# Sixteen of 31 convolution taps moved from VectorE to TensorE in a two-block fp32 model

## The chip, the cores and the metric

The kernel runs on one core of a Trainium2 chip. The metric is the device time of one launch in microseconds (us). Five engines run beside each other, each working through its own list of instructions in order: TensorE (PE; its weight loads are PEld), VectorE (DVE), ScalarE (ACT), GpSimd (POOL) and SyncE (SP), which only issues DMAs. An instruction that waits holds up all that stand behind it on its engine.

## The reference

Batch 1, 512 tokens (T), 1024 features, fp32. Two layers of a first block (each a mixer and a feed-forward part) are followed by one layer of a second block (two attention branches and a feed-forward part). The change touches the mixer's convolution branch alone:

```python
u = h @ w_in                                   # 1024 -> 4096
x_m, z, glu_a, glu_b = split(u, 4)             # 1024 channels each
...                                            # x_m, z: an mLSTM with 4 heads
a = glu_a * sigmoid(glu_b)
a = causal_depthwise_conv(a, w_dw, b_dw)       # 31 taps, each channel by itself
a = silu(group_layer_norm(a, 8, g_cn, b_cn))   # 8 groups of 128 channels
y = concat([h_m, a]) @ w_out
```

The convolution gives y[t] = b + sum over d = 0 to 30 of w[30 - d] * a[t - d], for each of 1024 channels.

## The kernel before

Products keep fp32 accuracy by splitting each operand into a rounded part and a remainder. `mm3` (L197 to L199) issues three matmuls for one product; a 128x512 result needs 24 of them. A weight unit is fetched by SP into one of two raw buffers `wr` (`fetch`, L170), rounded on ACT (L177) and its remainder taken on POOL (L179) or DVE (L68, through a helper that records all its instructions there), into one of four buffers `w`.

The order of the work is made in two steps. The code issues TensorE's products one after another and keeps a rough clock for TensorE (`pt`) and for VectorE (`dt`). After each product `pump` issues work in the background (generators that yield a cost on VectorE, an earliest time and a condition) while VectorE would not fall more than `slack` us behind TensorE. A list scheduler then fixes each engine's order by priorities; `later("tap")` puts the taps behind other work of VectorE.

In the mixer, feature tile c of the convolution (128 channels by 512 tokens, 8 tiles a layer) goes this way. Two products give glu_a and glu_b. ACT takes the tanh (L906), DVE writes the gated input `ga` (tile of three buffers). `conv_gen` (L819 to L832) has ACT write tap 0 with the bias into a bank of PSUM (L825; tag `py`, two banks), and DVE adds taps 1 to 30 there, one instruction each (L830). `conv_out` (L834 to L869) then copies the bank to SBUF (ACT, L839), turns it on TensorE (L846), takes the statistics and an inverse root on DVE (tile `cc`), norms on ACT (L858), turns it back on TensorE (L862) and applies the silu. The mLSTM's gates use fp32 matmuls without the split (`gates_mm`, L633): 128x32 weights by 512 columns into one of four groups of 32 PSUM partitions. Each such fp32 matmul shows as two rows in the trace. The 96 sums for the modulation (`ada_sum`, L287; 1024 columns each on VectorE, their tiles fetched by SP in the first mixer, by POOL after it) are background work of the first mixer and the first feed-forward part.

Of the kernel before, what the change touches and what calls it, by code (L numbers as in the profile page):

```python
# [7 lines left out]
F32 = mybir.dt.float32  # L8
# [9 lines left out]
KC, KM = 31, 4  # L18
EPS = 1e-6
# [11 lines left out]
COLS = {}  # L31
_o = 0
for _n, _w in (("g_pre_mix", 8), ("g_post_mix", 8), ("g_pre_mlp", 8), ("g_post_mlp", 8),
               ("b_ada", 48), ("w_conv_m", 8 * KM), ("b_conv_m", 8), ("g_mh", 8),
               ("w_dw", 8 * KC), ("b_dw", 8), ("g_cn", 8), ("b_cn", 8)):
    COLS[_n] = (_o, _w)
    _o += _w
NCOLS = _o
CONSTS = {"ident": (0, 128), "tri": (128, 128), "fold": (256, 8)}
NCONST = 264  # L40
# [4 lines left out]
# the guess is 1.5 ** 0.2 / sqrt, for the cubic step to have a leading coefficient of 1  # L45
# [8 lines left out]
class Paced:  # L54
    """an engine whose instructions are counted, by their rough time"""
# [16 lines left out]
class Kern:  # L72
    def __init__(self, ctx, tc, A, out, dump=None, stop=None):
# [13 lines left out]
        self.bufs = dict(E=8, s=12, e=1, t=5, tc=3, w=4, wr=2, hT=2, ga=3, z=2, c=26, cc=20, d=10, ad=4, j=2, gw=1, ga16=1)  # L87
# [44 lines left out]
    def pump(self):  # L132
        """issue what fits in before VectorE would be later than TensorE"""
# [12 lines left out]
    def drain(self, done):  # L146
        """issue background work until done()"""
# [11 lines left out]
    def add_chunk(self, src, widths, pool=""):  # L159
        """pool: which of the remainders GpSimd computes"""  # L160
        o = 0
        for i, w in enumerate(widths):
            self.plan.append((src[:, o:o + w], w, str(i) in pool))
            o += w
# [50 lines left out]
    def rsqrt(self, src, w, mul, add, tag=None):  # L215
        """1 / sqrt(src * mul + add), src [128, w]: a guess from the bits, a cubic and a quadratic step"""
# [30 lines left out]
    def setup(self):  # L247
# [8 lines left out]
        self.ones = self.K("tri")[:, 127:128].to_broadcast([128, 128])  # L256

    def load_cols(self, l):
# [10 lines left out]
        for n in ("w_conv_m", "b_conv_m", "w_dw", "g_cn", "b_cn", "g_mh"):  # L269
# [14 lines left out]
    def ada_sum(self, w, l, i):  # L284
        """mod[:, i] = w . silu(c), w the i-th 128 rows of w_ada^T"""
# [32 lines left out]
    def scale_cols(self, l, which):  # L318
        """g_pre * (1 + sc), and sh"""
# [7 lines left out]
    def gate_row(self, l, which):  # L327
        """gt * g_post, as a row on every partition"""
# [17 lines left out]
    def start(self, evacs):  # L346
        """the first normed operand by feature tile, as its scale and shift arrive, and the first products with it"""
# [91 lines left out]
    def norm_T(self, ii, xs, ss, G, sh, to):  # L439
        """rows of the token tiles from ii on, normed; transposed, scaled and split into hT two by two, as pend is worked off"""  # L440
# [48 lines left out]
    def feat(self, evacs, halves=False, hook=None, tag="p"):  # L489
        """128 outputs each: [128, T] = w^T h^T, handed to its evac"""  # L490
# [58 lines left out]
    def post_norm(self, l, which, nxt):  # L549
        """x += gt * rms_norm(y) * g_post; then the next normed operand"""  # L550
# [40 lines left out]
    def gate_weights(self, l):  # L591
        """Wq Wgq + Wk Wgk and Wv Wgv by head, as [feature, 8 gates]; in 4 steps"""
# [46 lines left out]
    def gates(self, l):  # L639
        """gate pre-activations by token -> log forget sums, and what the weights need; in 4 steps"""  # L640
# [89 lines left out]
    def weights_exp(self, h):  # L730
        """exp(a_s - M_t) for s <= t, by key tile"""
# [41 lines left out]
    def values(self, S, vt, h):  # L773
        """weighted sums of values, normed by head: [128 tokens, 4 tiles, 256]"""
# [41 lines left out]

    def conv_gen(self, l, inp, out):
        """the taps of the depthwise convolution, by channel tile"""
        nc, V = self.nc, self.nc.vector  # L819
        for c in range(8):  # L820
            yield 0, 0, lambda: c in inp and self.conv_out_at >= c - 1
            a, w = inp[c], self.cols[l]
            o = COLS["w_dw"][0] + c * KC + KC - 1
            y = self.bank(tag="py")
            nc.scalar.activation(y, a, AF.Identity, scale=w[:, o:o + 1], bias=self.col(l, "b_dw", c))  # L825
            yield 0, self.pt + 1, None
            for d in range(1, KC):
# [6 lines left out]
    def conv_out(self, l, c, yp, outs):  # L834
        """silu(norm over the 128 channels of the group)"""
# [3 lines left out]
        nc.scalar.activation(y, yp, AF.Copy)  # L839
# [220 lines left out]
    def tok_proj(self, n, kks, evac):  # L1060
        """[128 tokens, n] = h w for each token tile"""
# [27 lines left out]
    def rotate(self, src, i, n, pool=False):  # L1089
        """rotary embedding of n heads of token tile i; src and result [128, n, 64]"""  # L1090
# [14 lines left out]
    def q_hold(self, i, p, hold, tag):  # L1105
        """query heads of a token tile, rotated: [tokens, head, rounded part and remainder]"""
# [6 lines left out]
    def q_turn(self, i, hold, qt, hps):  # L1113
        """token tiles i and i + 1 of two pairs of heads into qt"""
# [18 lines left out]
    def q_proj(self, tag):  # L1133
        """8 query heads: 4 tiles [rounded part; remainder of a head, 2 heads, T], once the turns are worked off"""
# [5 lines left out]
    def k_proj(self):  # L1140
        """index key, 2 + 2 key heads: [part twice; T] for the rounded part and the remainder"""
# [61 lines left out]
    def qk_mm(self, out, q, h, tk, k, keys):  # L1203
        """q . k from [q_h; q_l] and [k_h; k_h], [k_l; k_l]"""
# [24 lines left out]
    def select(self):  # L1229
        """in place of the scores: 0 for each query's 128 largest (the earliest among equals), NEG elsewhere"""  # L1230
# [423 lines left out]
```

## Time and profile before

| | |
|---|---|
| time, median of 3 runs (lowest, highest) | 2427.93 us (2426.18, 2431.47) |
| profiled execution, first to last instruction | 2424.3 us |
| PE busy | 2252.7 us, 93% |
| DVE busy | 1610.0 us, 66% |
| ACT, POOL busy | 976.7 us, 625.4 us |
| matmul records | 10552 |

The page gives the profiled execution by its span, 2424.3 us; 3.6 us less than the median of the runs, which take in what lies around the span. In time the stages are: the start (0 to about 60 us), the first mixer (to about 464), its norm and feed-forward part (to 845), a norm (to about 890), the second mixer (to 1277), its norm and feed-forward part (to 1658), the second block's attention (to 2060) and feed-forward part. Busy shares over the whole span mix these stages; the rows below are by stage.

### The profile page before, as it was taken

The numbers are of one execution on the slowest core, as the hardware profiler recorded it, in microseconds if no ns is written. First come the engines' busy times: TensorE is split into PE (matmuls) and PEld (weight loads), VectorE is DVE, ScalarE is ACT, GpSimd is POOL, SyncE is SP. The second block draws the span as 40 slices with busy tenths as digits, with TensorE's granted clock in tenths as the row PEclk, the third lists the DMA queues.
The fourth block names the chain that finished last, engine by engine and source line by source line (L and its number), as shares of the span: only waits on it lengthen the run. The fifth ranks groups of instructions, "written<-read, shape, count | busy, mean of one in ns | idle before, by whom it ended". The sixth has DMA issues, their size and how long they took to land.

```text
span 2424.3 us, 28416 instructions
## 1 busy us (share of the span) xinstructions
PE 2252.7 (93%) x10552; PEld 1828.9 (75%) x10552; DVE 1610.0 (66%) x2971; ACT 976.7 (40%) x1705; POOL 625.4 (26%) x408
## 2 busy tenths in 40 slices
PE   5988998899999998898897999999989999999998
PEld 4667776688888776776676888887877888888886
DVE  6899999755777669999956233347887435443444
ACT  3434554443232343455445333234436543422332
POOL 2733452313234243444322011012031231000000
PEclk9999999999999999999998999999999999999999
DMA  7523223526666422222133332223111223322222
GB/s 271 174 75 106 71 81 118 181 97 214 214 206 205 144 97 81 66 66 66 63 108 104 122 104 96 96 87 109 62 70 44 63 103 138 110 95 94 95 96 87
DMA packets 77754, 271.34 MB, mean 112 GB/s; under 512 B 9008, under 2 KB 9776, under 8 KB 77616
## 3 DMA queue, kind: packets, MB, share of 16 engines
q1 hardware_dynamic: 69840, 241.21, 29.9%
q0 software_dynamic: 7776, 28.32, 3.6%
q8 instruction: 83, 1.36, 0.2%
q14 instruction: 55, 0.45, 0.1%
HBM read 256.91 MB, written 12.58 MB: 111 GB/s over the span
## 4 chain that ended last, share of the span: by engine, by line
PE 62%; DVE 24%; ACT 4%; issue 2%; POOL 1%; DMA 1%; ACTq 0%; DVEq 0%; SPq 0%; POOLq 0%
PE p L197 19%; PE p L199 19%; PE p L198 19%; DVE p L830 7%; DVE c L68 5%; DVE cc L68 2%; DVE t L68 2%; DVE s L68 1%; DVE E L68 1%; PE p L466 1%; DVE w L68 1%; DVE e L68 1%; DVE ad L287 1%; DVE d L68 1%; DVE hT L68 0%
## 5 line engine op out<-in xcount | busy, mean ns | idle before, releaser
L179 POOL TENSOR_TENSOR w<-wr,w 128x1024 fp32r<-128x1024 f32 (+1 forms) x166 | 399.7, 2411 | 842.8 <-ACT w L177 739.3
L177 ACT ACTIVATE w<-wr 128x1024 fp32r<-128x1024 f32 (+1 forms) x353 | 368.9, 1047 | 572.1 <-PE p L199 517.2
L197 PE MATMUL p<-hT,w 128*128 128x512 f32 (+1 forms) x1504 | 582.7, 389 | 14.0 <-ACT hT L209 7.6
L198 PE MATMUL p<-hT,w 128*128 128x512 f32 (+1 forms) x1504 | 576.0, 383 | 8.0 <-DVE hT L68 5.6
L199 PE MATMUL p<-hT,w 128*128 128x512 f32 (+1 forms) x1504 | 578.1, 385 | 1.3 <-POOL w L179 1.3
L197 PE MATMUL p<-w,s 128*128 128x512 f32 (+1 forms) x1152 | 450.9, 392 | 2.4 <-ACT s L209 2.2
L198 PE MATMUL p<-w,s 128*128 128x512 f32 (+1 forms) x1152 | 449.4, 390 | 2.0 <-DVE w L68 2.0
L199 PE MATMUL p<-w,s 128*128 128x512 f32 (+1 forms) x1152 | 447.3, 390 | 1.1 <-DVE s L68 0.8
L68 DVE TENSOR_TENSOR w<-wr,w 128x1024 fp32r<-128x1024 f32 (+1 forms) x187 | 232.9, 1245 | 288.2 <-ACT w L177 288.1
L197 PEld LDWEIGHTS p<-hT,w 128*128 128x128 f32 x1504 | 289.5, 193 | 74.5 <-ACT hT L209 9.6
L830 DVE SCALAR_TENSOR_TENSOR p<-ga,ad,p 128x495 f32<-128x495 f32 (+25 forms) x480 | 339.2, 728 | 3.3 <-ACT p L825 2.3
L198 PEld LDWEIGHTS p<-hT,w 128*128 128x128 f32 x1504 | 289.3, 192 | 64.9 <-DVE hT L68 7.5
L199 PEld LDWEIGHTS p<-hT,w 128*128 128x128 f32 x1504 | 289.3, 192 | 59.4 <-POOL w L179 3.3
L197 PEld LDWEIGHTS p<-w,s 128*128 128x128 f32 x1152 | 217.6, 189 | 52.3 <-ACT s L209 2.9
L199 PEld LDWEIGHTS p<-w,s 128*128 128x128 f32 x1152 | 217.4, 189 | 51.0 <-DVE s L68 1.2
L198 PEld LDWEIGHTS p<-w,s 128*128 128x128 f32 x1152 | 217.4, 189 | 49.6 <-DVE w L68 2.5
L68 DVE TENSOR_TENSOR E<-p,E 128x512 f32<-128x512 f32 (+4 forms) x152 | 95.3, 639 | 138.2 <-PE p L199 111.8
L68 DVE SCALAR_TENSOR_TENSOR t<-p,t 128x512 f32<-128x512 f32 x96 | 66.0, 687 | 129.6 <-ACT t L1028 129.6
L287 DVE SCALAR_TENSOR_TENSOR ad<-ad,ad 128x1024 f32<-128x1024 f32 x80 | 115.5, 1450 | 39.2 <-DMA ad<-in_ada_dram 39.1
L1028 ACT ACTIVATE t<-p 128x512 f32<-128x512 f32 x96 | 56.7, 591 | 179.7 <-PE p L199 179.7
L68 DVE TENSOR_TENSOR s<-t,s 128x512 fp32r<-128x512 f32 (+1 forms) x100 | 110.9, 1109 | 9.5 <-ACT s L1030 4.7
L573 POOL TENSOR_TENSOR E<-E,s 128x512 f32<-128x512 f32 x32 | 46.0, 1445 | 175.2 <-ACT j L571 175.2
(273 smaller groups left out, 2805.2 us busy)
## 6 DMA issues: line engine op xcount, KB each, us to landing
wr<-in_ff_dram SPq DMA_DIRECT2D x128, 512.0 KB, 3.7
wr<-in_win_dram SPq DMA_DIRECT2D x64, 512.0 KB, 3.6
ad<-in_ada_dram POOLq DMA_DIRECT2D x54, 512.0 KB, 4.8
wr<-in_wout_dram SPq DMA_DIRECT2D x40, 512.0 KB, 3.6
wr<-in_up_dram SPq DMA_DIRECT2D x32, 512.0 KB, 3.6
wr<-in_down_dram SPq DMA_DIRECT2D x32, 512.0 KB, 3.7
ad<-in_ada_dram SPq DMA_DIRECT2D x26, 512.0 KB, 4.2
xd<-E SPq DMA_DIRECT2D x20, 512.0 KB, 2.7
```

Of the source, the lines that this page charges most:

```text
L68: return f(out, *a, **kw)
L177: self.nc.scalar.activation(u[:, 0, :w], raw[:, :w], AF.Copy)
L179: eng.tensor_tensor(u[:, 1, :w], raw[:, :w], f32(u[:, 0, :w]), op=OP.subtract)
L197: mm(out, lh, rh, start=first, stop=False)
L198: mm(out, lh, rl, start=False, stop=False)
L199: self.mm = mm(out, ll, rh, start=False, stop=last)
L287: return self.nc.vector.scalar_tensor_tensor(w, w, 1.0, self.cact, op0=OP.mult, op1=OP.mult, accum_out=m)
L466: nc.tensor.transpose(p[:, k, 128 * t:128 * t + 128], x[t][:, j * 128:(j + 1) * 128], self.ident)
L573: nc.gpsimd.tensor_tensor(y[:, h], y[:, h], row[:, h], op=OP.mult)
L830: V.scalar_tensor_tensor(y[:, d:], a[:, :T - d], w[:, o - d:o - d + 1], y[:, d:], op0=OP.mult, op1=OP.add)
L1028: nc.scalar.activation(r, p, AF.Relu)
```

## The change

For each tile, SP copies `ga` 16 times from SBUF to SBUF into a new tile `shifts` [128, 4, 512]: for each of 4 shifts d and each of 4 groups g of 32 channels, partitions 32d to 32d + 31 of column block g get the group's 32 channels, d tokens late. `shifts` is one buffer for all tiles. POOL builds `cw` (two buffers), 16 blocks of 128x32: a stack of four 32x32 identities times the tap weights. Then 16 fp32 matmuls follow (4 sets m of 4 groups g; 128x32 weights by 512 - 4m columns), each for four taps of 32 channels, into the group's 32 partitions of the `py` bank. VectorE adds taps 16 to 30 behind them. ACT no longer writes tap 0; the bias moves into the copy of `conv_out`. The buffer from which POOL's DMAs take their descriptors shrinks to 2048 bytes a partition, which makes room for `shifts`. The rest of the diff takes out comments and docstrings, so line numbers shift by a few.

```diff
+CSETS = 4
+KV = KC - 4 * CSETS
...
-               ("w_dw", 8 * KC), ("b_dw", 8), ("g_cn", 8), ("b_cn", 8)):
+               ("w_dw", 8 * KV), ("w_pe", 32 * CSETS), ("b_dw", 8), ("g_cn", 8), ("b_cn", 8)):
...
+        self.shifts = self.const.tile([128, 4, T], F32, name="shifts")
+        nc.gpsimd.memset(self.shifts[:, :, 0:4], 0.0)
...
+    def conv_pe(self, l, inp, ys):
+        nc = self.nc
+        for c in range(8):
+            yield 0, 0, lambda: c in inp
+            for d in range(4):
+                for g in range(4):
+                    nc.sync.dma_start(self.shifts[32 * d:32 * d + 32, g, d:], inp[c][32 * g:32 * g + 32, :T - d])
+            w = self.tile("cw", (128, 4 * CSETS, 32))
+            nc.gpsimd.tensor_tensor(w, self.K("eye")[:, None, :].to_broadcast([128, 4 * CSETS, 32]),
+                                    self.col(l, "w_pe", c * 4 * CSETS, 4 * CSETS)[:, :, None].to_broadcast([128, 4 * CSETS, 32]),
+                                    op=OP.mult)
+            yield 0, self.pt + 6, lambda: self.conv_out_at >= c - 1
+            y = self.bank(tag="py")
+            for m in range(CSETS):
+                for g in range(4):
+                    nc.tensor.matmul(y[32 * g:32 * g + 32, 4 * m:], w[:, 4 * m + g, :], self.shifts[:, g, :T - 4 * m],
+                                     start=m == 0, stop=m == CSETS - 1)
+            self.pt += 0.853 * CSETS
+            ys[c] = y
+
     def conv_gen(self, l, inp, out):
-        nc, V = self.nc, self.nc.vector
+        V = self.nc.vector
+        ys = {}
+        self.spawn(self.conv_pe(l, inp, ys), front=True)
         for c in range(8):
-            yield 0, 0, lambda: c in inp and self.conv_out_at >= c - 1
-            a, w = inp[c], self.cols[l]
-            o = COLS["w_dw"][0] + c * KC + KC - 1
-            y = self.bank(tag="py")
-            nc.scalar.activation(y, a, AF.Identity, scale=w[:, o:o + 1], bias=self.col(l, "b_dw", c))
+            yield 0, 0, lambda: c in ys
             yield 0, self.pt + 1, None
-            for d in range(1, KC):
+            a, w, y = inp[c], self.cols[l], ys[c]
+            o = COLS["w_dw"][0] + c * KV + KC - 1
+            for d in range(4 * CSETS, KC):
                 yield 0.06 + (T - d) / 860, 0, None
                 with self.later("tap"):
                     V.scalar_tensor_tensor(y[:, d:], a[:, :T - d], w[:, o - d:o - d + 1], y[:, d:], op0=OP.mult, op1=OP.add)
...
-        nc.scalar.activation(y, yp, AF.Copy)
+        nc.scalar.activation(y, yp, AF.Identity, bias=self.col(l, "b_dw", c))
...
-    nc = bacc.Bacc("TRN2", target_bir_lowering=False, num_devices=1)
+    nc = bacc.Bacc("TRN2", target_bir_lowering=False, num_devices=1, dynamic_dma_scratch_size=2048)
```

The scheduler decides where the new instructions land. TensorE, first mixer, the product of glu_a for the third tile, before (`p_925`; `hT` and `w` are its split operands):

```order
L197 MATMUL p_925<-hT_66,w_749 128x512
L198 MATMUL p_925<-hT_67,w_749 128x512
L199 MATMUL p_925<-hT_66,w_749 128x512
L197 MATMUL p_925<-hT_66,w_749 128x512
L198 MATMUL p_925<-hT_67,w_749 128x512
```

The same product now (`p_985`; L199 to L201 are the three matmuls), with the second tile's convolution (`p_889`, L838) in it:

```order
L838 MATMUL p_889<-shifts,cw_836 32x512 x2
L200 MATMUL p_985<-hT_67,w_774 128x512
L201 MATMUL p_985<-hT_66,w_774 128x512
L199 MATMUL p_985<-hT_66,w_774 128x512
L838 MATMUL p_889<-shifts,cw_836 32x512
L200 MATMUL p_985<-hT_67,w_774 128x512
L201 MATMUL p_985<-hT_66,w_774 128x512
L199 MATMUL p_985<-hT_66,w_774 128x512
L838 MATMUL p_889<-shifts,cw_836 32x512
L838 MATMUL p_889<-shifts,cw_836 32x508 x4
L838 MATMUL p_889<-shifts,cw_836 32x504 x4
L838 MATMUL p_889<-shifts,cw_836 32x500 x4
```

The first set of four stands in three pieces (2, 1 and 1 matmuls), three matmuls of the product between them; only the other three sets follow in one piece.

SP's list about there, before (`wr` are weight units, `ad` tiles of the modulation):

```order
L170 DMA wr_786<-in_qkv_dram 128x512
L298 DMA ad_3568<-in_ada_dram 128x1024
L170 DMA wr_847<-in_win_dram 128x1024
L170 DMA wr_923<-in_win_dram 128x1024
L170 DMA wr_1005<-in_win_dram 128x1024
```

And now, with the copies of the second tile (`ga_809`):

```order
L829 DMA shifts<-ga_809 32x512
L172 DMA wr_814<-in_qkv_dram 128x512
L829 DMA shifts<-ga_809 32x512 x3
L829 DMA shifts<-ga_809 32x511 x4
L829 DMA shifts<-ga_809 32x510
L172 DMA wr_877<-in_win_dram 128x1024
L829 DMA shifts<-ga_809 32x510 x3
L829 DMA shifts<-ga_809 32x509 x4
```

Sixteen copies stand between or ahead of the weight fetches of the same time.

VectorE in the first mixer, before, where the taps of two tiles (`p_792`, `p_461`) alternate:

```order
L830 SCALAR_TENSOR_TENSOR p_792<-ga_781,ad_91,p_792 128x511
L830 SCALAR_TENSOR_TENSOR p_461<-ga_421,ad_91,p_461 128x488
L830 SCALAR_TENSOR_TENSOR p_792<-ga_781,ad_91,p_792 128x510
L830 SCALAR_TENSOR_TENSOR p_461<-ga_421,ad_91,p_461 128x487
L68 SCALAR_TENSOR_TENSOR t_835<-E_832,ad_91,t_835 128x511
```

And the second tile's taps now (`p_889`), beginning with tap 16, between sums of the modulation (L291):

```order
L856 SCALAR_TENSOR_TENSOR p_889<-ga_809,ad_93,p_889 128x496
L291 SCALAR_TENSOR_TENSOR ad_784,mod_104<-ad_784,ad_90 128x1024
L856 SCALAR_TENSOR_TENSOR p_889<-ga_809,ad_93,p_889 128x495
L291 SCALAR_TENSOR_TENSOR ad_845,mod_104<-ad_845,ad_90 128x1024
L856 SCALAR_TENSOR_TENSOR p_889<-ga_809,ad_93,p_889 128x494
```

Of the modulation's tiles SP now fetches 43 in the first mixer instead of 26, POOL 37 instead of 54: as many sums move from the feed-forward part into the mixer.

## Rows read from the trace of the kernel before

**Rows 1.** Busy time by stretch; columns in the first row, (x) counts instructions.
```profile
core 0: us, PE busy (x) PEld busy (x) DVE busy (x) ACT busy (x) POOL busy (x), PEclk, DMA share, GB/s
60.00:464.00 404.00, 363.48 (x1682) 283.50 (x1681) 369.53 (x724) 189.64 (x352) 168.53 (x107) 0.95 0.36 117
500.00:845.00 345.00, 344.10 (x1526) 280.87 (x1524) 225.80 (x275) 110.82 (x154) 110.09 (x89) 1.00 0.58 185
890.00:1277.00 387.00, 351.19 (x1660) 281.42 (x1659) 340.66 (x669) 178.08 (x333) 160.59 (x112) 0.97 0.24 77
1658.00:2060.00 402.00, 378.73 (x1986) 315.61 (x1985) 266.45 (x704) 199.87 (x441) 89.61 (x54) 0.97 0.25 83
```

**Rows 2.** The chain of waits by line, 60 to 464 us, shares of the stretch.
```profile
by line: DVE p L830 17.3%; DVE c L68 7.1%; PE p L197 6.8%; PE p L199 6.7%; PE p L198 6.6%; DVE cc L68 5.3%; DVE s L68 3.7%; DVE ad L287 3.4%; issue 2.9%; DMA ad<-in_ada_dram 2.7%; DVE d L68 2.3%; ACT tc L858 1.4%; DVE E L68 1.3%; DVE e L68 
```

**Rows 3.** The same chain by line, 890 to 1277 us.
```profile
by line: DVE p L830 25.5%; DVE cc L68 9.3%; DVE t L68 8.1%; PE p L199 7.9%; PE p L198 7.6%; DVE c L68 7.6%; PE p L197 7.6%; DVE s L68 5.2%; issue 2.7%; DVE E L68 2.1%; DVE e L68 1.6%; ACT tc L858 1.4%; ACT t L892 1.0%; DVE ga L68 1.0%; DVE 
```

**Rows 4.** TensorE's waits, 60 to 464 us: total us, times, longest.
```profile
PE p L862 <- ACT tc L858: 6.8, 5, 2.6
PE p L669 <- DVE d L68: 6.3, 1, 6.3
PE p L810 <- ACT E L802: 5.7, 1, 5.7
PE p L612 <- DMA ga<-in_wqT_dram: 3.9, 1, 3.9
```

**Rows 5.** TensorE's waits, 890 to 1277 us.
```profile
PE p L862 <- ACT tc L858: 15.1, 7, 3.2
PE p L810 <- ACT E L802: 7.5, 2, 4.9
PE p L633 <- DVE E L68: 7.0, 1, 7.0
```

**Rows 6.** Groups by line and shape: busy us, mean ns, idle before.
```profile
L830 DVE SCALAR_TENSOR_TENSOR p<-ga,ad,p 128x511 f32<-128x511 f32 x16 | 11.9, 743 | 2.3 <-ACT p L825 2.3
...
L830 DVE SCALAR_TENSOR_TENSOR p<-ga,ad,p 128x497 f32<-128x497 f32 x16 | 11.6, 728 | 0.1
```

**Rows 7.** The page's costliest groups, the modulation's sums.
```profile
L287 DVE SCALAR_TENSOR_TENSOR ad<-ad,ad 128x1024 f32<-128x1024 f32 x80 | 115.5, 1450 | 39.2 <-DMA ad<-in_ada_dram 39.1
```

**Rows 8.** TensorE in order of time: start us, us, instruction, count.
```profile
123.33 0.40 PE L199 MATMUL p<-hT,w 128*128 128x512 f32 x1
123.66 3.62 PE L633 MATMUL p<-E,gw 128*32 128x512 f32 x26
...
129.28 1.05 PE L633 MATMUL p<-E,gw 128*32 128x512 f32 x4 [2.00 <-POOL E L895]
...
130.60 0.39 PE L198 MATMUL p<-hT,w 128*128 128x512 f32 x1
...
956.62 0.39 PE L199 MATMUL p<-hT,w 128*128 128x512 f32 x1
956.84 0.40 PE L197 MATMUL p<-hT,w 128*128 128x512 f32 x1
957.17 1.04 PE L633 MATMUL p<-E,gw 128*32 128x512 f32 x2
958.15 0.50 PE L198 MATMUL p<-hT,w 128*128 128x512 f32 x1
958.49 0.39 PE L199 MATMUL p<-hT,w 128*128 128x512 f32 x1
```

**Rows 9.** SP's issues at the start, in order of time.
```profile
0.81 1.81 SPq L361 DMA_DIRECT2D s<-in_x_dram  x4
```

**Rows 10.** DMA issues, 60 to 464 us: count, KB each, us to landing.
```profile
wr<-in_win_dram SPq DMA_DIRECT2D x26, 512.0 KB, 3.6
wr<-in_qkv_dram SPq DMA_DIRECT2D x4, 256.0 KB, 2.7
```

**Rows 11.** POOL in order of time, one 128x512 instruction with two inputs.
```profile
951.73 1.42 POOL L179 TENSOR_TENSOR w<-wr,w 128x512 fp32r<-128x512 f32 x1 [5.62 <-ACT w L177]
```

More of the change, by code (lines that the diff above doesn't have):

```diff
@@ L38 @@
 NCOLS = _o
-CONSTS = {"ident": (0, 128), "tri": (128, 128), "fold": (256, 8)}
-NCONST = 264
+CONSTS = {"ident": (0, 128), "tri": (128, 128), "fold": (256, 8), "eye": (264, 32)}
+NCONST = 296
 NEG = -1e30
@@ L86, in __init__ @@
         self.n = 0
-        self.bufs = dict(E=8, s=12, e=1, t=5, tc=3, w=4, wr=2, hT=2, ga=3, z=2, c=26, cc=20, d=10, ad=4, j=2, gw=1, ga16=1)
+        self.bufs = dict(E=8, s=12, e=1, t=5, tc=3, w=4, wr=2, hT=2, ga=3, z=2, c=26, cc=20, d=10, ad=4, j=2, gw=1, ga16=1, cw=2)
         self.plan, self.units, self.next, self.prepped = [], {}, 0, 0
@@ L268, in load_cols @@
         self.bgr[l] = b
-        for n in ("w_conv_m", "b_conv_m", "w_dw", "g_cn", "b_cn", "g_mh"):
+        for n in ("w_conv_m", "b_conv_m", "w_dw", "w_pe", "g_cn", "b_cn", "g_mh"):
             o, w = COLS[n]
@@ L1564, in consts @@
             c[32 * g + i, o + i] = 1.0
+    o = CONSTS["eye"][0]
+    for g in range(4):
+        c[32 * g:32 * g + 32, o:o + 32] = np.eye(32)
     return c
@@ L1589, in layout @@
         for n in COLS:
-            v = I[n][l]
-            if n in ("w_conv_m", "w_dw"):
+            v = I["w_dw" if n == "w_pe" else n][l]
+            if n == "w_dw":
+                v = v[:KV]
+            if n == "w_pe":
+                v = v[::-1][:4 * CSETS].reshape(CSETS, 4, 8, 4, 32).transpose(1, 4, 2, 0, 3)
+                cols.append(v.reshape(128, -1))
+            elif n in ("w_conv_m", "w_dw"):
                 cols.append(v.reshape(v.shape[0], 8, 128).transpose(2, 1, 0).reshape(128, -1))
```

## The prediction, made before the changed kernel ran

> **What bounds the kernel now.** I read busy time by stretch first [rows 1]. The two mixers (60 to 464 us, 890 to 1277 us) are the stretches that the change touches. In them VectorE is busy for 369.5 of 404 us (91%) and 340.7 of 387 us (88%), TensorE for 363.5 and 351.2 us. In the feed-forward part beside them (500 to 845 us) VectorE has 65% and TensorE never stops: 344.1 of 345 us. So in the mixers neither engine has much room, and both must be counted.
>
> The chain of waits says which one ends last [rows 2, 3]. In both mixers its largest line is the taps (L830): 17.3% of 404 us is 70 us, 25.5% of 387 us is 99 us; most other lines of it are VectorE's too. The mixers are VectorE-bound, so taking taps off VectorE takes work off the path. TensorE's own waits fit [rows 4, 5]: it waits for the copy after the convolution's norm (L862, 6.8 and 15.1 us), for the mLSTM's norm (L810, 5.7 and 7.5 us), for the gates (L669 6.3, L633 7.0 us), and each of these comes through VectorE's list.
>
> How much can a faster VectorE give back? What TensorE loses there. Its granted clock is one of two levels, 2.4 GHz (1.00) or 1.2 GHz (0.50), and the means of 0.95 and 0.97 [rows 1] are stretches at the low level, behind waits. I take TensorE's work at full clock as its busy time less the low clock's part. First mixer: 363.5 - 0.05 x 404 = 343.3 us, so 60.7 us are lost. Second: 351.2 - 0.03 x 387 = 339.6 us, 47.4 us lost. Together 682.9 us of work, 108.1 us lost (76.3 idle, 31.8 low clock), in 791 us. That 108 us is the most the relief can be worth.
>
> **What goes from VectorE.** 15 taps x 16 tiles; a tap takes 743 ns at 511 columns and 728 ns at 497 [rows 6], so 15 x 0.735 x 8 = 88 us a mixer. In the first mixer 17 sums of the modulation come in from the feed-forward part, 17 x 1.45 = 25 us [rows 7], because the planner now sees room; in the feed-forward part they were hidden under TensorE, so nothing is won there. VectorE is left with 369.5 - 88 + 25 = 306 us and 340.7 - 88 = 253 us, 74% and 62% of mixers some 410 us long. It no longer bounds them.
>
> **What comes to TensorE.** The gates' fp32 matmuls (L633) have the same shape, 128x32 weights by 512 columns into four groups of PSUM partitions [rows 8].
> - In one piece: 26 records (13 matmuls of two records) take 3.62 us. One after the other they would take 13 x 0.86 us, so the four groups do run beside each other. 13 matmuls are what stands in one piece in nearly all tiles of the new order: the last of set 0 and sets 1 to 3.
> - Alone: from 956.84 to 958.49 us is 1.65 us where two spacings of the product (0.23 each) would stand, so one lone matmul costs 1.19 us. A pair, from 129.28 to 130.60 us, takes 1.32 us; the lone one from 957.17 to 958.49 us also 1.32. A pair costs what one costs, 1.19 us.
> - The way in and out is 1.19 - 1.04 = 0.15 us more than the record, so the piece of 13 costs 3.77 us.
>
> The order cuts set 0 into 2, 1 and 1 in 13 of 16 tiles: 1.19 + 1.19 + 3.77 = 6.15 us. The first tile has three lone ones, 7.34 us; one tile of the second mixer has its sets cut in the middle (2.38 + 2 x 2.05 = 6.48 us) and one a piece more (7.34 us). Sum: 13 x 6.15 + 7.34 + 6.48 + 7.34 = 101 us, half in each mixer. This is the term that decides, and it lies on an engine that will now be the bound: 682.9 + 101 = 784 us of TensorE's work against 791 us that the mixers take today.
>
> Rows 8 also show what a switch costs: the spacing into L633 is 0.33 instead of 0.23 us, and the first spacings behind it are longer too. The Trainium skill (TensorEngine Tiling (Array Packing), Tiling Modes) says that a change of the tiling mode drains TensorE, which speaks against cutting a set into pieces. The trace agrees with a small number, the 0.15 us and the slow restart that the 1.19 us hold; with no drain three pieces would cost 2 x 0.86 + 3.44 = 5.16 us a tile, 83 us in all, and the sum would be 18 us less.
>
> **What stays lost.** Bounds: the feed-forward part loses 0.9 us at 65% VectorE, but has no long chains; the attention (1658 to 2060 us, 66% VectorE, many chains) loses 402 - (378.7 - 0.03 x 402) = 35 us, 9%. For two mixers that is 2 to 71 us, with 108 us as the end where the relief gives nothing. Half of the taps' 169 us on the chain go, 84 us, more than the 72 us idle behind VectorE (76.3 less the 3.9 us on a DMA [rows 4]). On average VectorE is then early; but waits come in bursts, behind 20 small instructions of an inverse root or the short convolution's taps, which stay. I keep a third, 24 us, the 3.9 us, and of the low clock its share, 31.8 x 28 / 76 = 12 us: 40 us.
>
> **The copies.** 16 issues on SP at 0.45 us, as four take 1.81 us [rows 9], are 7.2 us; the nearest landing is 2.7 us for 256 KB, against 64 KB here [rows 10]; with tanh and gating before them some 11.5 us from the end of glu_b's product. In the new order the first matmul of the convolution stands 16 to 22 us of product rows behind that end in 13 tiles, but 10.7, 12.7 and 13.9 us in three. I take 3 us in all; bounds 0 and, if SP's list is held by a fetch ahead, the third rival. Behind the copies weight fetches wait up to 7.2 us; four converted units of 24 matmuls (5.5 us each) cover that. POOL's 16 products at 1.42 us each by the nearest row [rows 11] and ACT's saving of a pass a tile lie beside TensorE: POOL is 42% busy, ACT 47% [rows 1].
>
> **Sum.** 682.9 + 101 + 40 + 3 = 827 us for the two mixers instead of 791: +36 us. The span goes from 2424.3 to 2460.3 us; with 3.6 us around it, as now, 2464 us. VectorE gets its relief, and TensorE pays more for it than it got back: slower.
>
> **Rivals.**
> 1. TensorE's price is lower, or nothing stays lost: faster. If cut sets cost no more than whole ones, 16 x 3.77 = 60 us: 682.9 + 60 + 40 + 3 = 786, -5 us, 2423 us. Or all waits vanish as in the feed-forward part: 682.9 + 101 + 2 = 786, the same time. For it: VectorE falls to that part's share. Against: the measured lone matmul, and chains that the feed-forward part lacks. It decides once price and loss together are under 100 us (105 us is no change). 12%.
> 2. The relief gives nothing back: chains of small instructions, not the taps, hold TensorE. 108 us stay lost: +104 us, 2532 us. Against: the taps' share of the chain. 8%.
> 3. The copies come late. SP works in order, and a fetch ahead of the copies waits for a raw buffer, which waits for TensorE's progress. At 4 us a tile, less than one unit's 5.5 us, 16 tiles add 64 us: 2528 us. For it: fetches stand among the copies. Against: the distance above. 15%.
>
> **Chances.** The forecast has 65%, its own range 2439 to 2495 us (15 to 71 us lost). A measurement of this kernel tells 0.2%, 4.9 us, from no change. Faster: the first rival, 12%; the same: the edge between it and the forecast, 6%; slower: 82%. The range reaches to the first rival's edge below, and above to the greater part of the third: 2424 to 2512 us.
>
> **What would show it.** Right: matmul records of L838 (32 a tile, 512 in all) at 6 us of TensorE a tile; VectorE at 74% and 62% in the mixers; the waits of L862 and L810 a third of now; the chain of waits led by TensorE's products in place of the taps; the first mixer some 12 us longer, the second some 24 us. Wrong: a wait of L838 for DMAs above 1 us a tile (third rival); L862's wait as long as now (second); mixers shorter than 404 and 387 us (first).

## The result, and the profile after

The changed kernel takes 2530.59 us (median of 4 runs, 2527.66 to 2534.18) against 2427.05 us for the kernel before on the same chip: a ratio of 1.0426, 95% interval 1.0409 to 1.0443, or 104 us more. The forecast was 2464 us. The direction is right; the time lies above the whole range and 1.4 us from the second rival's. One execution of one experiment (e11, 2590.79 us) ran in a slower state of the chip and is left out below.

The line numbers move: mm3 is now L199 to L201, the taps L856, the copies L829, the convolution's matmuls L838, the two turns of `conv_out` L872 and L888, the modulation's sums L291. Busy time by stretch, the four stretches that answer to [rows 1]:

```profile
60.00:528.00 468.00, 418.79 (x1949) 296.55 (x1947) 316.99 (x640) 187.93 (x347) 175.82 (x115) 0.93 0.46 138
564.00:908.00 344.00, 343.08 (x1523) 280.34 (x1521) 189.81 (x239) 110.70 (x154) 97.89 (x72) 1.00 0.50 159
954.00:1377.00 423.00, 397.66 (x1905) 286.60 (x1904) 260.56 (x547) 171.55 (x322) 165.77 (x116) 0.98 0.33 91
1759.00:2161.00 402.00, 380.13 (x1985) 317.90 (x1986) 265.51 (x702) 199.50 (x440) 88.92 (x54) 0.97 0.26 83
```

The feed-forward part and the attention take what they took; all of the loss is in the two mixers, 64 us in the first and 36 us in the second. VectorE has fallen to 68% and 62% there (forecast 74% and 62%; in the first it is busy for 317 us against 306, in a longer mixer). By the prediction's own reckoning TensorE's work at full clock is 418.8 - 0.07 x 468 = 386.0 and 397.7 - 0.02 x 423 = 389.2 us, 775 us in all: 92 us more than before (forecast 101). What TensorE loses is 468 - 386.0 = 82.0 and 423 - 389.2 = 33.8 us, 116 us in all: it was 108 and should have come down to 43, the copies' 3 us included. So the work came about as priced, and the relief gave nothing back.

The bounds of these stretches are not the same products before and after, by some ten of TensorE's matmuls. Cut at the same products (the kernel before so cut stands at e1 below) the mixers of the changed kernel are:

```profile
55.00:549.00 494.00, 434.88 (x2022) 310.14 (x2022) 336.96 (x676) 198.05 (x363) 188.98 (x121) 0.93 0.45 134
970.00:1400.00 430.00, 394.91 (x1901) 284.88 (x1900) 266.41 (x565) 172.78 (x325) 164.72 (x113) 0.96 0.32 89
```

So cut, the mixers are 62 and 40 us longer, and the loss is 93.7 and 52.3 us against 71.8 and 59.8 us before: 22 us more in the first mixer, 7 us less in the second. The clock is given to 0.01, so a loss is known to some 2.5 us. The sum says the same as above, that nothing came back; the share of the second mixer depends on the cut.

The chain of waits, by line, first and second mixer (answering [rows 2, 3]):

```profile
by line: PE p L199 11.0%; PE p L200 10.6%; PE p L838 10.4%; PE p L201 10.2%; issue 8.4%; DVE ad L291 7.6%; DVE p L856 6.9%; DVE cc L70 5.0%; POOL w L181 3.2%; DMA ad<-in_ada_dram 3.1%; DVE s L70 2.5%; DVE t L70 2.1%; DVE c L70 1.7%; DVE d L
...
by line: PE p L199 14.0%; PE p L201 13.7%; PE p L200 13.6%; PE p L838 9.8%; issue 5.1%; DVE p L856 4.1%; DVE c L70 3.9%; POOL w L181 3.9%; DVE cc L70 3.1%; DMA shifts<-ga 3.0%; DVE t L70 2.8%; DMA wr<-in_win_dram 2.2%; DVE d L70 2.2%; DVE s
```

TensorE's products now lead it, and the taps fell from 17.3 to 6.9% and from 25.5 to 4.1%. In the first mixer the modulation's sums went from 3.4 to 7.6%. TensorE's waits, first mixer and then second (answering [rows 4, 5]; total us, times, longest):

```profile
PE p L888 <- ACT tc L884: 12.8, 4, 7.0
PE p L872 <- ACT tc L865: 11.9, 2, 8.7
PE p L838 <- DMA shifts<-ga: 5.5, 2, 4.5
...
PE p L838 <- DMA shifts<-ga: 8.4, 3, 4.9
PE p L888 <- ACT tc L884: 5.4, 4, 1.6
```

In the first mixer the wait for the norm's copy (L888; L862 in [rows 4]) did not shrink to a third of 6.8 us but rose to 12.8 us, which the prediction named as the mark of the second rival; in the second mixer it fell from 15.1 to 5.4 us. The wait for the mLSTM's norm (L814 now; L810 in [rows 4, 5], 5.7 and 7.5 us) did go, to 0.9 us in the second mixer, and is not listed in the first. New are the waits for the copies (with one put down to a weight fetch 15.5 us in both mixers, just under the 1 us a tile that was to be the third rival's mark) and the 11.9 us for the first turn (L872).

The longest of those can be followed back through VectorE and ScalarE (an instruction's idle time before it, and what ended it, in brackets):

```profile
149.57 0.74 DVE L856 SCALAR_TENSOR_TENSOR p<-ga,ad,p 128x496 f32<-128x496 f32 x1 [8.57 <-PE p L838]
150.22 1.53 DVE L291 SCALAR_TENSOR_TENSOR ad<-ad,ad 128x1024 f32<-128x1024 f32 x1
...
174.67 0.71 DVE L856 SCALAR_TENSOR_TENSOR p<-ga,ad,p 128x482 f32<-128x482 f32 x1
176.21 1.12 PE L872 MATMUL p<-identr,tc 128*128 128x128 f32 x4 [8.72 <-ACT tc L865]
```

VectorE stood 8.6 us until the tile's matmuls were done. Its 15 taps, 11 us by themselves, then took from 149.6 to 175.4 us, because four sums of the modulation and many small instructions stand between them; then TensorE stood 8.7 us for the copy of the finished tile. The change put the copies and the matmuls ahead of the taps, and the planner put sums among them.

The convolution's matmuls by shape (busy us, mean ns, idle before; two records are one matmul):

```profile
L838 PE MATMUL p<-shifts,cw 128*32 128x512 f32 x128 | 59.2, 683 | 15.5 <-DMA shifts<-ga 13.9 <-DMA wr<-in_win_dram 1.7
L838 PE MATMUL p<-shifts,cw 128*32 128x508 f32 x128 | 30.3, 598 | 0.0
```

One tile of them, and TensorE's products beside it, in order of time (start us, us, instruction, count):

```profile
185.05 0.40 PE L199 MATMUL p<-hT,w 128*128 128x512 f32 x1
185.38 1.05 PE L838 MATMUL p<-shifts,cw 128*32 128x512 f32 x2
186.35 0.51 PE L200 MATMUL p<-hT,w 128*128 128x512 f32 x1
...
187.17 0.60 PE L888 MATMUL p<-identr,tc 128*128 128x128 f32 x4
187.69 3.58 PE L838 MATMUL p<-shifts,cw 128*32 128x512 f32 x26
191.21 0.51 PE L200 MATMUL p<-hT,w 128*128 128x512 f32 x1
```

The price by shape is as read from the gates' matmuls [rows 8]: 1.05 us for a lone matmul, 3.58 us for a piece of 13 (a piece is what stands in TensorE's order with no product between). All 512 records take 100.1 us (the forecast's 101). The set that is cut, the one with 512 columns, costs twice each of the others.

The copies on SP in order of time (answering [rows 9]):

```profile
228.09 9.14 SPq L829 DMA_DIRECT2D shifts<-ga  x10
242.23 0.33 SPq L172 DMA_DIRECT2D wr<-in_win_dram  x1
242.60 3.90 SPq L829 DMA_DIRECT2D shifts<-ga  x6
```

Their landing by shape, first mixer (count, KB each, median us; answering [rows 10]):

```profile
shifts<-ga SPq DMA_DIRECT2D x32, 64.0 KB, 4.3
shifts<-ga SPq DMA_DIRECT2D x32, 63.9 KB, 3.6
shifts<-ga SPq DMA_DIRECT2D x32, 63.8 KB, 2.1
```

Six copies take 3.90 us, 0.65 us each where the estimate had 0.45 (the first ten hold a wait of 2.9 us as well). Behind the first ten SP stands 5 us at a weight fetch before it issues the other six; the profile gives that wait as one for POOL, which has to finish with the raw buffer:

```profile
SPq L172 <- POOL w L181: 4.9, 1, 4.9
```

That is the third rival's mechanism, at a smaller price: TensorE's wait for this tile's copies is 1.06 us. The Trainium skill (DMA: Bandwidth & Descriptors, Anatomy of one DMA — SWDGE (gpsimd) path) says that a semaphore wait happens on the issuing sequencer and not in the DMA engines. These rows, of SP and not of the GpSimd path, agree in that the wait stands in the issuer's list.

### The profile page after: what moved, and what is told of

Its sections match the earlier page's. It is cut to its first block, busy times and chain, and to the rows that moved or that the text cites. A ratio compares the mean times of both kernels' runs of the same rounds, so it can differ in the third digit from the quotient of the medians.

```text
span 2525.9 us, 29607 instructions
## 1 busy us (share of the span) xinstructions
PE 2354.1 (93%) x11064; PEld 1846.4 (73%) x11064; DVE 1444.7 (57%) x2733; ACT 968.4 (38%) x1689; POOL 630.6 (25%) x408
## 3 DMA queue, kind: packets, MB, share of 16 engines
q1 hardware_dynamic: 84576, 266.89, 33.8%
## 4 chain that ended last, share of the span: by engine, by line
PE 70%; DVE 16%; ACT 5%; issue 4%; POOL 3%; DMA 2%; SPq 0%; ACTq 0%; DVEq 0%; POOLq 0%
PE p L199 20%; PE p L200 20%; PE p L201 20%; DVE c L70 4%; PE p L838 4%; DVE p L856 2%; DVE cc L70 1%; DVE ad L291 1%; POOL w L181 1%; DVE t L70 1%; PE p L470 1%; DVE E L70 1%; DVE s L70 1%; DMA shifts<-ga 1%; DVE d L70 1%
## 5 line engine op out<-in xcount | busy, mean ns | idle before, releaser
L199 PE MATMUL p<-hT,w 128*128 128x512 f32 (+1 forms) x1504 | 582.6, 389 | 19.1 <-ACT hT L211 8.8
L201 PE MATMUL p<-hT,w 128*128 128x512 f32 (+1 forms) x1504 | 578.6, 385 | 1.5 <-POOL w L181 1.5
L199 PE MATMUL p<-w,s 128*128 128x512 f32 (+1 forms) x1152 | 451.6, 392 | 6.1 <-ACT s L211 2.6
L201 PE MATMUL p<-w,s 128*128 128x512 f32 (+1 forms) x1152 | 449.6, 391 | 0.5 <-POOL s L212 0.5
L199 PEld LDWEIGHTS p<-hT,w 128*128 128x128 f32 x1504 | 289.2, 193 | 89.1 <-ACT hT L211 11.5
L201 PEld LDWEIGHTS p<-hT,w 128*128 128x128 f32 x1504 | 288.6, 192 | 63.0 <-issue 6.6
L199 PEld LDWEIGHTS p<-w,s 128*128 128x128 f32 x1152 | 219.0, 190 | 58.4 <-ACT s L211 3.4
L201 PEld LDWEIGHTS p<-w,s 128*128 128x128 f32 x1152 | 218.5, 190 | 50.6 <-issue 1.4
L856 DVE SCALAR_TENSOR_TENSOR p<-ga,ad,p 128x496 f32<-128x496 f32 (+14 forms) x240 | 173.9, 725 | 57.0 <-PE p L838 52.5
L291 DVE SCALAR_TENSOR_TENSOR ad<-ad,ad 128x1024 f32<-128x1024 f32 x80 | 114.7, 1437 | 44.1 <-DMA ad<-in_ada_dram 44.1
L838 PE MATMUL p<-shifts,cw 128*32 128x500 f32 (+3 forms) x512 | 100.1, 613 | 15.5 <-DMA shifts<-ga 13.9
L70 DVE TENSOR_TENSOR s<-t,s 128x512 fp32r<-128x512 f32 (+1 forms) x100 | 106.9, 1069 | 12.8 <-ACT s L1056 8.2
```

The costliest lines, as they stand in the source:

```text
L70: return f(out, *a, **kw)
L199: mm(out, lh, rh, start=first, stop=False)
L201: self.mm = mm(out, ll, rh, start=False, stop=last)
L291: return self.nc.vector.scalar_tensor_tensor(w, w, 1.0, self.cact, op0=OP.mult, op1=OP.mult, accum_out=m)
L838: nc.tensor.matmul(y[32 * g:32 * g + 32, 4 * m:], w[:, 4 * m + g, :], self.shifts[:, g, :T - 4 * m], start=m == 0, stop=m == CSETS - 1)
L856: V.scalar_tensor_tensor(y[:, d:], a[:, :T - d], w[:, o - d:o - d + 1], y[:, d:], op0=OP.mult, op1=OP.add)
```

## The experiments

All times are medians in groups that share a chip with the kernel before (2425.9 to 2428.2 us in the groups). "Ahead" and "behind" by stage are the start of the same product's matmul in two traces.

**The parts by themselves.** e1 has the relief alone, leaving taps 1 to 15 out:

```diff
 # conv_gen of the kernel before
-for d in range(1, KC):
+for d in range(16, KC):
 ...
```

> The kernel before without taps 1 to 15 (left out, nothing takes their place): the relief of VectorE alone. Theory A (the relief is real, as the prediction had it: what TensorE loses in the two mixers falls from 108 to about 40 us): 2427 - 68, about 2360 us. Rival B (the relief gives nothing back, chains of small instructions hold TensorE): about 2427 us, and the waits of L862 as before.

2443.83 us, ratio 1.0067 (1.0048 to 1.0086). With 240 taps fewer the kernel is 18 us slower. Busy time by stretch of the kernel before and of e1, between the same products of each mixer:

```profile
53.00:485.00 432.00, 381.78 (x1766) 298.63 (x1765) 389.51 (x756) 201.71 (x371) 182.31 (x113) 0.95 0.35 113
907.00:1297.00 390.00, 345.82 (x1648) 278.08 (x1647) 342.61 (x684) 178.83 (x335) 157.18 (x107) 0.96 0.24 77
```

```profile
53.00:497.00 444.00, 386.57 (x1768) 304.07 (x1767) 329.83 (x653) 200.76 (x371) 183.44 (x113) 0.93 0.37 119
921.00:1321.00 400.00, 355.19 (x1647) 285.60 (x1646) 270.94 (x567) 178.32 (x335) 156.72 (x107) 0.94 0.24 75
```

VectorE does 131 us less in the two mixers (732 to 601), and TensorE loses more, not less: 131.6 us before and 157.3 us in e1, idle time and low clock together (50.2 + 0.05 x 432, and so on). So the relief by itself, as the planner uses it, does not bring TensorE's loss down, as the prediction's step "on average VectorE is then early" had it. The chain of waits of e1's first mixer says what came in the taps' place:

```profile
by line: PE p L197 12.5%; PE p L198 11.8%; PE p L199 11.7%; DMA ad<-in_ada_dram 8.1%; DVE c L68 6.7%; DVE ad L287 6.5%; DVE p L830 5.4%; DVE cc L68 5.1%; issue 5.0%; POOL w L179 3.0%; DVE s L68 2.5%; DVE t L68 2.0%; PE p L810 1.1%; ACT w L1
```

Against [rows 2], a slightly shorter stretch, the taps are down from 17.3 to 5.4%, but the sums and their fetches are up from 6.1 to 14.6%; 32 sums stand in this mixer in place of 24.

e6 has the matmuls alone: `KV = KC`, taps from 1 on VectorE, no copies, the staging tile zeroed once.

> The changed kernel's matmuls on a staging tile that is zeroed once (no copies), with taps 1 to 30 left on VectorE (tap 0 is left out): the price of the matmuls without copies and without relief. If TensorE is the bound and its added 73 us of busy time (as without copies) come on top one for one: 2490 to 2505 us. If the run of the relief alone (+18) and the run without copies (+53) simply add: 2426 + 35 = 2461 us. If VectorE, now as loaded as before, also delays the accumulators: over 2510 us.

2465.68 us, 1.0164 (1.0147 to 1.0180): +38 us, for 63 us of matmuls, near the 2461 us at which the runs were expected to add.

```profile
55.00:513.00 458.00, 416.20 (x2072) 306.39 (x2071) 392.88 (x764) 196.99 (x363) 189.21 (x122) 0.96 0.34 107
932.00:1336.00 404.00, 369.36 (x1843) 282.28 (x1843) 329.39 (x686) 173.49 (x327) 162.68 (x111) 0.96 0.24 74
```

TensorE's work rises by 61 us (690.4 to 751.1) and its loss falls from 131.6 to 110.9: a third of the matmuls' time fell into what TensorE would have lost anyway. Pieces of several lengths stand in this trace:

```profile
406.71 1.04 PE L835 MATMUL p<-shifts,cw 128*32 128x512 f32 x2
408.27 1.06 PE L835 MATMUL p<-shifts,cw 128*32 128x512 f32 x8
444.06 1.90 PE L835 MATMUL p<-shifts,cw 128*32 128x508 f32 x16
1057.13 2.73 PE L835 MATMUL p<-shifts,cw 128*32 128x508 f32 x22
```

A lone matmul (2 records) takes as long as four (8 records), one in each column group. Eight take 1.90, eleven 2.73 and sixteen 3.60 us. So the time goes by rounds of up to four matmuls, 0.85 us a round, with 0.2 us more for a piece.

e8 has the copies alone, issued in the kernel before into a tile that nothing reads.

> The kernel before, all 31 taps on VectorE, with the 256 copies added on SP's queue into a tile that nothing reads (and the smaller scratch of the changed kernel): the price of the copies by themselves, 256 issues of 0.63 us in SP's order and 17 MB of small transfers. If the copies cost through SP's order and the traffic (late weights and ada tiles): 2440 to 2455 us. If they cost only where TensorE waits for them: 2422 to 2432 us.

2427.81 us, 1.0003 (0.9993 to 1.0013). In that kernel 256 issues and their traffic cost nothing where nobody waits for them.

**Parts taken out of the changed kernel.** e2 drops the copies; the staging tile is zeroed once, so the matmuls add zeros.

> The changed kernel without the 256 copies into shifts (left out; the tile is zeroed once, the matmuls read it). Theory A (late copies, through SP's list, cost what is lost beyond the forecast): what stays lost falls from 116 to about 45 us, and the sets stand whole more often, some 25 us less work: 2530 - 95, about 2435 us. Rival B (relief gives nothing): only the fewer pieces, 2505 us.

2478.75 us, 1.0219 (1.0204 to 1.0234): +53 us, between its two theories and about e1 and e6 together (18 + 38). Its matmuls stand in 30 pieces (53 in the changed kernel), 72.4 us.

e4 keeps the copies and holds a set's first matmuls until all 16 have landed, so that the scheduler can't begin on the first four channel groups:

```diff
 ...
+    if m == 0:
+        for copy in copies:
+            self.tc.add_manual_dep(i.ins, copy.ins.name, SYNC, reason="whole")
```

> The changed kernel with the four matmuls of set 0 made to wait for the tile's last copy, so that all 16 stand in one piece in 13 of 16 tiles. If pieces cost what the prediction says (1.19 us a lone matmul or pair): TensorE's records of L838 fall from 100 us to about 62 us, and the time by 38 us to 2492 us. Rival: the later start gives it back as waits for copies, 2510 to 2530 us.

2502.75 us, 1.0317 (1.0299 to 1.0335): 28 us less than the changed kernel, where 38 were expected. The matmuls stand in 19 pieces:

```profile
L838 PE MATMUL p<-shifts,cw 128*32 128x500 f32 (+3 forms) x512 | 66.3, 638 | 12.9 <-DMA shifts<-ga 8.0 <-DMA ga<-in_wqT_dram 4.7 <-issue 0.3
```

A tile in order of time:

```profile
183.03 3.60 PE L838 MATMUL p<-shifts,cw 128*32 128x512 f32 x32
```

The same 512 records take 66.3 us in place of 100.1: 33.8 us for 34 cuts, 1.0 us each. Most of that is not the change between two kinds of matmul. By e6's rows a piece of 2, one of 1 and one of 13 matmuls take 1 + 1 + 4 rounds where a whole set of 16 takes 4, so a cut costs one round more, 0.85 us, in which three or two column groups stand empty; the piece of 16 takes no longer than the piece of 13 did (3.60 and 3.58 us). The change itself is left with 0.2 us: two pieces of 16 records would take 3.80 us where one of 32 takes 3.60. The Trainium skill (TensorEngine Tiling (Array Packing), Tiling Modes) says that a change of the tiling mode drains TensorE; the runs leave room for such a drain of about 0.2 us a piece by these records (0.34 us by the prediction's 1.19 for a lone one, which counts the slower products around it), and not for 1 us.

e3 leaves the cuts and changes only what the planner charges for a tap, that is the time on VectorE that `pump` books for it:

```diff
-yield 0.06 + (T - d) / 860, 0, None
+yield 2 * (0.06 + (T - d) / 860), 0, None
```

> The changed kernel with each tap's cost in the planner doubled, so that the planner sees as much work on VectorE as before and SP fetches 26 tiles of the modulation in the first mixer, not 43. Theory C (the 17 sums and fetches moved into the first mixer cause the loss there, 82 us instead of 61 before): 30 to 45 us less, 2485 to 2500 us, all of it in the first mixer. Theory A (the copies alone): 2525 to 2535 us.

2502.81 us, 1.0318 (1.0302 to 1.0333), again 28 us less, with 24 sums in the first mixer as before. The whole gain is in the first mixer (63 us behind the kernel before at its end in the changed kernel, 34 in e3).

**Both cures, and the relief well paced.** e7 is e3 and e4 in one.

> The changed kernel with both cures, the planner charging a tap twice and a set's matmuls held until all 16 copies have landed. If each took away a cost of its own (28 and 28 us): 2475 us. If both cures worked on the same waits: 2492 to 2505 us. Under 2426 only if the relief, well paced, gives over 60 us back.

2471.97 us, 1.0192 (1.0171 to 1.0213): the two gains add, to 3 us. The cures take away different costs.

e5 is e1 with the charge doubled.

> The kernel before without taps 1 to 15 (as in the run of the relief alone), but with the planner charging each of the 15 remaining taps twice, so that it plans VectorE as full as before while VectorE really does half. Theory P (the relief alone came out 18 us slower because the planner pulls other VectorE work, ada sums above all, forward into the time that was freed): 2385 to 2412 us, 15 to 40 us under the kernel before, with 26 ada tiles in the first mixer again and not 34. Theory Q (what TensorE loses in the mixers is chains of small dependent steps, which a freer VectorE does not shorten): 2420 to 2435 us, whatever the planner charges.

2408.77 us, 0.9929 (0.9912 to 0.9946). That is in theory P's range: 35 us lie between e1 and e5, which run the same taps. The charge moves sums (24 stand in the mixer again) and spreads the taps; this run doesn't tell the two apart.

```profile
53.00:470.00 417.00, 377.91 (x1766) 298.48 (x1765) 306.99 (x639) 200.72 (x371) 182.74 (x113) 0.96 0.37 117
892.00:1281.00 389.00, 348.84 (x1649) 280.37 (x1648) 271.60 (x567) 179.09 (x336) 157.60 (x107) 0.95 0.25 77
```

Yet this is the most that the relief gave in any run: with VectorE at 74% and 70% TensorE still loses 115.4 us, 16 us less than the kernel before at 90% and 88%.

e11 is the control, the kernel before with all its taps and a charge of 1.25.

> Control for the well-paced relief (2409 us): the kernel before with all its 31 taps on VectorE and each charged 1.25 times in the plan. If the pacing by itself gave the 19 us: 2400 to 2415 us. If VectorE has to be relieved for it: 2424 to 2445 us, the taps now ending too late.

2481.45 us, 1.0224 (1.0197 to 1.0250). This slower plan without relief costs 54 us, so a higher charge is not a gain by itself. Other charges of this kernel were not tried.

**What the planner did with the room.** e10 takes e4 and doubles the least distance between two of the modulation's sums.

> The changed kernel with the matmuls held for all 16 copies (2503 us) and the planner's least distance between two ada sums doubled (33 of them fall into the first mixer in place of 43), the taps charged as in the changed kernel. If the price of the unpaced relief is the ada sums that are pulled into the mixer: 2470 to 2480 us, as with the doubled charge. If it is the density of the taps themselves on VectorE: 2495 to 2505 us.

2503.80 us, 1.0312 (1.0282 to 1.0342): no gain, by this run the sums are not it. Its trace says otherwise: it is 16 us ahead of e4 at the end of the first mixer and gives 15 us back at the end of the feed-forward part, where the wider distance held too and the last sums came late. e12 widens it in the first mixer's settings alone:

```diff
-TUNE = [dict(slack=8.0, tap=50, ..., gap=6.0, ...
+TUNE = [dict(slack=8.0, tap=50, ..., gap=12.0, ...
```

> The changed kernel with the matmuls held for all 16 copies (2503 us) and the planner's least distance between two ada sums doubled in the first mixer alone. If the ada sums pulled into the first mixer are what the unpaced relief pays for there: 16 us less by the end of that mixer and none of it given back in the feed-forward stage, 2484 to 2490 us. If the sums that were put off cost the same wherever they run: 2498 to 2506 us.

2491.24 us, 1.0263 (1.0247 to 1.0280): 12 us less than e4 by the medians. In the two profiled executions (spans 2488.6 and 2507.1 us; e4's is its slowest) it is 19 us ahead at the first mixer's end and still 20 us at the end of the second. VectorE's sums in the first mixer, in the kernel before, in the changed kernel, in e4 and in e12:

```profile
L287 DVE SCALAR_TENSOR_TENSOR ad<-ad,ad 128x1024 f32<-128x1024 f32 x24 | 33.5, 1394 | 4.5 <-DMA ad<-in_ada_dram 4.4
```

```profile
L291 DVE SCALAR_TENSOR_TENSOR ad<-ad,ad 128x1024 f32<-128x1024 f32 x41 | 59.4, 1449 | 6.6 <-DMA ad<-in_ada_dram 6.6
```

```profile
L292 DVE SCALAR_TENSOR_TENSOR ad<-ad,ad 128x1024 f32<-128x1024 f32 x41 | 57.0, 1391 | 10.7 <-DMA ad<-in_ada_dram 10.6
L292 DVE SCALAR_TENSOR_TENSOR ad<-ad,ad 128x1024 f32<-128x1024 f32 x26 | 35.6, 1368 | 8.4 <-DMA ad<-in_ada_dram 8.4
```

The sums were pulled from the feed-forward part, where TensorE hides them, into the mixer, where TensorE waits for VectorE's list. They stand on SP's list as well. SP's waits in the first mixer for a sum's buffer to come free, before, changed, e12:

```profile
SPq L298 <- DVE ad L287: 32.4, 15, 7.0
```

```profile
SPq L302 <- DVE ad L291: 95.0, 20, 13.5
```

```profile
SPq L303 <- DVE ad L292: 38.9, 11, 8.5
```

**What the copies cost.** e9 is e7 with the matmuls placed 16 us of the plan behind the copies (6 before).

> The changed kernel with both cures (taps charged twice, a set's matmuls held for all 16 copies; 2472 us), and with the matmuls placed 16 us of the plan behind the copies in place of 6. The parts measured so far (matmuls alone +38, relief well paced -19) leave 25 us of this kernel's +45 to the wait for the copies. If that is lateness alone: 2445 to 2455 us. If the copies are late because they stand in SP's order behind fetches that themselves wait, so that a later matmul meets as late a copy, or if a convolution that comes later only moves the wait to the mixers' ends: 2465 to 2485 us.

2466.86 us, 1.0159 (1.0128 to 1.0191), 5 us less than e7 with runs from 2456.9 to 2471.3: within their spread, a small gain at most.

e13 is e3 without copies.

> The changed kernel with taps charged twice and no copies (the matmuls read a staging tile that is zeroed once). If the parts add (matmuls alone +38, relief well paced -19): 2443 to 2450 us, and 25 us of the 2472 us with both cures are the wait for copies. If the matmuls cost more once VectorE's waits are gone: 2455 to 2470 us, and the copies cost little.

2460.68 us, 1.0138 (1.0123 to 1.0153), in the range of its second theory. The parts do not add here: 19 us were expected (38 - 19), 33 came. e13 differs from e6 by the well-paced relief alone and is only 5 us shorter, with intervals that overlap (its matmuls, cut a little more, take 69.3 us against 63.0). So beside the matmuls, which had already filled 21 us of TensorE's loss, the relief gives little, and unpaced it costs 13 us (e2 less e6). The copies cost 11 us in the paced kernel (e7 less e13) and 24 us in the unpaced one (e4 less e2). Both figures are net, for the kernels without copies have more cuts (e2's matmuls take 6 us more than e4's). In e4 TensorE's own waits in front of the convolution's matmuls are 12.9 us; where the rest of the 24 us stands was not followed.

**Fewer taps on TensorE.** e14 and e15 set CSETS to 2 and 1 in e9 (8 and 4 taps), with a charge of 1.3 and 1.1.

> 8 taps on TensorE in place of 16 (two sets of matmuls, the same 16 copies), a set held for all its copies, placed 16 us of the plan behind them, the 23 taps left charged 1.3 times, so that the plan is as full as before. If the price is in proportion (half of 38 and of -19, and the wait for the copies): 2436 to 2446 us. If TensorE's own waits swallow the first 20 us of the matmuls' 31 (as they did with 25 of 63 in the run of the matmuls alone): 2422 to 2432 us, level with the kernel before or under it.

> 4 taps on TensorE (one set of matmuls, the same 16 copies), the rest as with 8 taps and the 27 taps left charged 1.1 times. In proportion: 2431 to 2438 us. If TensorE's waits swallow all of the matmuls' 16 us: 2418 to 2428 us.

2448.57 us, 1.0091 (1.0075 to 1.0107), and 2440.21 us, 1.0047 (1.0030 to 1.0063), 2 to 3 us above the ranges that go by proportion. The price comes down with the share but does not reach zero (the 16 copies a tile stay), and no share tried beats the kernel before. Of the kernels that compute the whole model it stays the fastest, level with e8; e5 beats it only by leaving taps out.

## Why the prediction was wrong

Where the 104 us come from, by differences of runs:

| part | measured | from | forecast |
|---|---|---|---|
| matmuls nearly in whole sets, no relief | +38 us | e6 | +60 |
| the cuts | +28 us | changed less e4 | +41 |
| the relief as the planner uses it | +18 us | e1 | -68 |
| the wait for the copies | +24 us | e4 less e2 | +3 |
| sum | +108 us (measured +104) | | +36 |

The sum closes almost by construction: the cuts and the copies are the two steps from the changed kernel down to e2. What it tests is that e1 and e6 add up to e2 (56 and 53 us). In the paced kernels the parts do not add (e13).

- **TensorE's price: right.** 100.1 us of matmuls against 101, the cuts and the pieces of 13 included, and 1.05 us for a lone one. At full clock the same 53 pieces would take about 94 us by e6's rows (an estimate), and the forecast's 101 less its 0.15 us a piece is 93. As time the price is less, 38 + 28 = 66 us, because part of it falls where TensorE would have stood anyway (e6). The prediction added all of it to the work and looked for the relief in the loss, so this part of the return was there in it, under the wrong name.
- **"What stays lost", 40 us: this step failed.** 116 us stayed. It held that half the taps' share of the chain, 84 us, exceeds TensorE's idle time behind VectorE, so that VectorE would be early and two thirds of the waits would go. The relief by itself gave 19 us at most (e5), 5 us beside the matmuls (e13 and e6), and as the planner of the changed kernel uses it -18 (e1). The chain of waits was misread. A line's share of it tells what stood on the chain, and not how much shorter the chain is without it: the planner fills VectorE's list up to TensorE's own plan, and with the taps out other work stood there, the sums and their fetches at 14.6% in e1 and 10.7% in the changed kernel.
- **"17 sums come in, nothing is won there": the count was right (24 to 41), the price was not.** They were priced at their 25 us of VectorE and at nothing for TensorE. Keeping 15 of the 17 out of the mixer is worth 12 us (e12). With the doubled charge, which keeps the sums out too and spreads the taps, it is 28 to 35 us (changed less e3, e4 less e7, e1 less e5). What the other part is made of, the taps' density in the list or the order that comes of it, was not separated.
- **The copies, 3 us: mis-sized, the mechanism as in the third rival.** 11 to 24 us in place of 3 or of that rival's 64. Issue was 0.65 us and not 0.45, landing 2.1 to 4.3 us, and SP stood at a fetch among them. Copies from another engine's queue were not tried. A longer distance in the plan helped little (e9), as it would if the copies stand behind a fetch that itself waits; that was not shown further.
- **The second mixer went the forecast's way, but not as far**: no sums to pull in, the work up by 49.6 us, L888's wait down to a third, the loss down by 14 us (7 us cut at the same products) where the forecast needed some 27 (half of 101 less the 24 us by which the mixer was to grow). It grew by 36 us. So part of the miss is there too, and not only in the sums.
- **The rivals.** The second, with 8%, gave 2532 us and was the case: the relief gives nothing back. That it comes within 1.4 us is in part luck: the mixers' work grew by 92 us and not by 101, and 116 us stay lost, not 108 and 3 for the copies. Its reason, chains of small instructions, is not shown: e5 shows that TensorE goes on losing 115 us with VectorE at 74% and 70%, but what holds it there was not taken apart. e1 shows that on top the plan turns room into other work.

## What to carry to other kernels

Before an engine is relieved, ask what will fill the room: where a planner feeds that engine by its own cost model, the freed time goes to other background work, and work that was hidden elsewhere moves into the stretch that is short. The share of the chain that a line holds is no measure of what its removal gives back; run the removal alone, without its price, as the first experiment. Ask also whether two gains draw on the same waits: here the new matmuls and the relief both drew on TensorE's lost time, and together they gave back less than each alone. On TensorE, matmuls that run side by side in column groups belong in full rounds, behind a wait for all their inputs: a lone one takes the time of four.

## What the runs showed of the hardware

- Fp32 matmuls of 128x32 weights by 512 columns in four column groups run side by side, in rounds: a piece of one or of four took 1.04 to 1.06 us, of eight 1.90, of eleven 2.73, of sixteen 3.60 us (e6, e4). A cut that leaves a lone matmul so cost 1.0 us (33.8 us for 34 cuts), a cut at a full round 0.2 us by the same rows.
- 256 extra SBUF-to-SBUF copies of 64 KB cost 0.4 us in all, within noise, where nothing read them (e8), and 11 to 24 us where TensorE did (e7 less e13, e4 less e2). The issue took 0.65 us each, more than the 0.45 us of a 512 KB load [rows 9].
- 61 us more of TensorE's work cost 38 us (e6): the idle time and the time at the low clock fell from 131.6 to 110.9 us, the mean granted clock of the mixers staying at 0.96 (0.95 and 0.96 before).
